# The expert stage of a two-block layer: no subtractions on GpSimd, half the down products in fp32, three tiles' results added by one-hot products ahead of a branch

## The chip, the cores and the metric

One core of a Trainium2 chip runs the whole program: an attention and feed-forward block of two layers, then a second block that ends in a mixture of experts. The metric is the device time of one execution in microseconds. The change touches only the last stage, the experts and what follows them.

## The reference, cut to what matters

512 tokens of width 1024. Each token has one group of four experts and, in it, two experts of inner width 256:

```
g_weight, g_idx = top_k(softmax(x @ w_group + b_group), 1)
e_val, e_idx    = top_k((x @ w_router + b_router)[g_idx], 2)
e_weight        = softmax(e_val) * g_weight
combine[n, e]   = e_weight of expert e for token n, else 0
act = silu(x @ w_gate[e]) * (x @ w_up[e]) * combine[:, e]      # for 16 experts
out = sum over e of act @ w_down[e]
h = h + out;  result = rms_norm(h, norm_final_g)
```

All of it is in float32.

## The kernel before, in words

The kernel computes only the chosen pairs. `route` ranks the 1024 (token, expert) pairs into tiles of 128 rows: tiles 0 to 15 are the first 128 rows of each expert, 16 to 18 hold overflow of experts that got more (their expert is known at run time alone, so their weights come by indirect DMAs that POOL issues), 19 to 22 exist under a branch (`tc.If(rv > 3)`) that these inputs do not take. The order of the tiles is 0 to 9, 16, 17, 18, 10 to 15.

Each tile runs through `moe`: its 128 token rows are gathered from DRAM (`xg`, an indirect DMA of POOL), transposed (`xgp`) and split; six weight chunks of 512 KB (128x1024 floats) come in, four for gate and up, two for down; `up` makes 24 products into one bank (`gups`), ACT applies SiLU (`ma<-gups`), DVE multiplies by weight and up part (`ma`), PE transposes that (`mat`), and `down` makes 12 products (`mdps`). Down of a tile is written after up of the next one.

A product is exact enough only when both sides are split: an fp32 value becomes hi (fp32r, which PE takes in one pass) and lo = value - hi. ACT copies the hi part (`whi`, for down chunks `whx`), a subtraction makes lo (`wlo`, `wlx`), and `mm3` (lines 297 to 299) makes hi*hi, hi*lo and lo*hi. Before the change, of each static tile's six weight subtractions two run on POOL, one of the up chunks and one of the down chunks (in the last tile one in all); the rest are on DVE, for tiles 16 to 18 all six.

The result of a tile (`yt`) is taken from its banks half by ACT, half by DVE (`K.ev` alternates) and written to DRAM (`yb`, an ACT queue DMA). Tiles 14 and 15 (`fin`) are not written: their result stays in SBUF (`yf`, split), and a one-hot matrix `fS` (made by `scatter_from` in the middle of the stage) spreads it over the tokens by products (`fsc`). After the last `moe` step POOL gathers the other results back, eight indirect DMAs of 512 KB (`yg`, one per 128 tokens and choice); then come the branch, the sums into `x` (DVE, POOL, and for two of the token blocks PE through the identity), and the final norm.

Weights are requested 18 chunks ahead (`wstream`) by SP's queue; their buffers are nine `raw` ones and pages of a common pool of 26 (`rawp`, also `xg`, `xgt`, `whx`, `wlx`, `yt`, `yf`, `yg`). A scheduler orders the instructions of each engine by a modelled timeline and inserts the semaphores; on the chip each engine and each DMA queue then runs its list in order. At the branch every engine reads the register and waits for what it needs of the others; nothing is moved across it.

Of the kernel before, what the change touches and what calls it, by code (L numbers as in the profile page):

```python
# [253 lines left out]
class Kern:  # L254
# [1485 lines left out]
    def second_tail(K, mix, xs):  # L1740
        nc, A = K.nc, K.A
        mo = K.pg([128, 512], F32, "moec")
        nc.sync.dma_start(mo, A["moec"])
        wr = K.pg([128, 8, 20], F32, "wrt")
        nc.sync.dma_start(wr.rearrange("p k n -> p (k n)"), A["wrt"])
        nc.gpsimd.tensor_tensor(wr, wr, K.v("gf2").unsqueeze(2).to_broadcast([128, 8, 20]), op=ALU.mult)
        K.eqm = K.rp.tile([128, 256], BF16, name="eqm")
        nc.scalar.activation(K.eqm, mo[:, 128:384], AF.Copy)
        lg = K.rp.tile([128, 4, 20], F32, name="rlg")
        G = K.row(A["grow"][1:2], "gfin")  # L1750
        gf = K.row(A["grow"][0:1], "gf2")
        xnd = K.dp.tile([512, 1024], F32, name="xnd")
        K.yb = [K.dp.tile([n * 128 + 1, 1024], F32, name=f"yb{n}") for n in (17, 4)]
        z = K.pg([1, 1024], F32, "zrow")
        nc.gpsimd.memset(z, 0.0)
        for n, y in zip((17, 4), K.yb):
            nc.scalar.dma_start(y[n * 128:n * 128 + 1, :], z)
        lt = K.bank([128, 4, 20], name="rtp", tag="r")
        K.phase("wout2")
        ws = [K.wconv(t, False) for t in K.w2raw]  # L1760
        ro = K.branch_norm(1)
        K.wstream(5)
        for tb in range(4):
            K.out2(xs[tb], mix, 4, tb, ws, ro[:, tb:tb + 1])
            K.route_in(xs[tb], tb, gf, xnd, wr, lt, lg)
        K.phase('route')
        K.wstream(K.WDEPTH)
        idx, wrow, pos, tl, sl, wsl, nov = K.route(lg, mo)
        K.phase('moe')
        K.wrow = wrow  # L1770
        fin = K.order[-2:]
        S = K.pg([128, 2, 4, 128], F32R, "fS")
        T = {}

        def scatter_from():

            io = mo[:, 0:128]
            for z, j in enumerate(fin):
                m, u = K.rp.tile([128, 2, 4], F32, name=f"fm{z}"), K.rp.tile([128, 4], F32, name=f"fu{z}")
                nc.vector.tensor_scalar(m, tl, float(j), None, op0=ALU.is_equal)  # L1780
                t = K.rp.tile([128, 2, 4], F32, name=f"ft{z}")
                nc.vector.scalar_tensor_tensor(t, sl, 1.0, m, op0=ALU.add, op1=ALU.mult)
                nc.vector.tensor_tensor(u, t[:, 0], t[:, 1], op=ALU.add)
                nc.vector.tensor_scalar(u, u, 1.0, None, op0=ALU.subtract)
# [6 lines left out]
                K.ev(S[:, z], ps)  # L1791
# [12 lines left out]
        def part(ps, tb, h, z):  # L1804
            for p in range(2):
                nc.tensor.matmul(ps, S[:, z, tb], T[z][p][:, h * 512:h * 512 + 512], start=(z == 0 and p == 0), stop=(z == 1 and p == 1 and tb > 1))

        ts = []
        K.moe(K.order, xnd, idx, wsl, K.wnext, fin, T, scatter_from, lambda: ts.extend(gather(0)))
        rv = nc.values_load(nov[0:1, 0:1], min_val=0, max_val=7)  # L1810
        with K.tc.If(rv > 3):
            for j in range(19, 23):
                K.moe([j], xnd, idx, wsl)
            for t in gather(1):
                add(*t)
        for tb in (2, 3):
            nc.gpsimd.tensor_tensor(xs[tb], xs[tb], ts[2 * tb][0], op=ALU.add)
        for tb in range(4):
            t = ts[2 * tb + 1][0]
            if tb > 1:  # L1820
                nc.vector.tensor_tensor(xs[tb], xs[tb], t, op=ALU.add)
            else:
                nc.vector.tensor_tensor(xs[tb], xs[tb], ts[2 * tb][0], op=ALU.add)
            for h in range(2):
                ps = K.bank([128, 512], name="fsc", tag=("T", "g", "b", "T")[tb])
                c = slice(h * 512, h * 512 + 512)
                part(ps, tb, h, 0)
                part(ps, tb, h, 1)
                if tb < 2:
                    nc.tensor.matmul(ps, K.ident, t[:, c], start=False, stop=True)  # L1830
                nc.vector.tensor_tensor(xs[tb][:, c], xs[tb][:, c], ps, op=ALU.add)
        K.phase('final')
        for tb in range(4):
            ss = K.sm([128, 1], "fss")
            K.sumsq(xs[tb], ss)
            r = K.rsqrt(ss, 1, 1.0 / D, EPS, "fr")
            if tb < 0:
                nc.gpsimd.tensor_tensor(xs[tb], xs[tb], G, op=ALU.mult)
                nc.scalar.activation(xs[tb], xs[tb], AF.Copy, scale=r)
            else:  # L1840
                nc.vector.scalar_tensor_tensor(xs[tb], xs[tb], r, G, op0=ALU.mult, op1=ALU.mult)
# [21 lines left out]
    def route(K, lg, mo):  # L1863
# [129 lines left out]
        Z = (17 * 128.0, 4 * 128.0)  # L1993
# [3 lines left out]
        stt(m[:, 0], tl, 13.5, u, op0=ALU.is_lt, op1=ALU.add)  # L1997
        ts(m[:, 1], tl, 18.5, None, op0=ALU.is_gt)
        pi2 = sm([2, 2, 4], "rpos", I32)
        stt(u, u, -256.0, p, op0=ALU.mult, op1=ALU.add)  # L2000
        for z, (q, d) in enumerate(((u, 0.0), (p, 19 * 128.0))):
            stt(m[:, z], q, Z[z] + d, m[:, z], op0=ALU.subtract, op1=ALU.mult)
            ts(pi2[:, z], m[:, z], Z[z], None, op0=ALU.add)
# [21 lines left out]
            K.wq.append((c, j, K.wraw(j, c)))  # L2025
            K.wn += 1

    def wconv(K, raw, pool, pg=False):
        nc = K.nc
        if pg:  # L2030
            hi, lo = K.pg([128, 1024], F32R, "whx"), K.pg([128, 1024], F32R, "wlx")
# [21 lines left out]
    def moe(K, tiles, xnd, idx, wsl, weights=None, fin=(), T=None, mid=None, rest=None):  # L2053

        nc, A = K.nc, K.A
        if not weights:
            def weights(j, cs):
                return [K.wconv(K.wraw(j, c), False) for c in cs]

        def load(j):  # L2060
            x = K.page(j, "xg")
# [19 lines left out]
            nc.vector.scalar_tensor_tensor(a, a, wsl[:, j:j + 1], ps[:, 256:512], op0=ALU.mult, op1=ALU.mult)  # L2081
            return a

        def act(a):
            pt = K.bank([128, 2, 128], name="mat", tag="T")
            for k in range(2):
                nc.tensor.transpose(pt[:, k], a[:, k * 128:k * 128 + 128], K.ident)
            s = K.t2([128, 2, 2, 128], "mas", F32R)
            K.split(s[:, 0], s[:, 1], pt)
            return s  # L2090

        def down(j, s, w):
# [4 lines left out]
            for h in range(2):  # L2097
                c = slice(h * 512, h * 512 + 512)
                ps = K.bank([128, 512], name="mdps", tag="b")
                for k in range(2):  # L2100
                    K.mm3(ps, (s[:, 0, k], s[:, 1, k]), (w[k][0][:, c], w[k][1][:, c]), k == 0, k == 1)
# [12 lines left out]
        for i, j in enumerate(tiles):  # L2114
# [53 lines left out]
```

## Time and profile before

| | |
|---|---|
| time, median of 3 runs | 2298.61 us (2293.86 to 2303.5) |
| the profiled execution | 2302.42 us, span 2300.6 us |
| busy over the span | PE 92%, DVE 64%, ACT 44%, POOL 15% |
| first product of the expert stage | 2043.9 us |
| last up product done | 2257.2 us |
| from there to the end of the span | 43.4 us |

Times in the views are us from the start of the span, durations us unless marked ns. In a timeline the bracket is the idle time of the engine ahead of the instruction and what ended it; "x2" are merged instructions, with one duration over all. PE's products are pipelined, so their starts tell the pace, not their durations. A clock of 1.00 is PE's full speed. `L2036` is line 2036 of the listing.

### The profile page before, as it was taken

The page shows a single profiled execution, that of the slowest core. Times are in us where ns is not written, and L with a number is a line of the kernel's source. Part 1 is how long each engine was busy: PE and PEld are TensorE (multiplying, and loading weights), DVE is VectorE, ACT ScalarE, POOL GpSimd, SP SyncE. Part 2 cuts the span into 40 slices and gives each one's busy share as a digit, 9 for nine tenths or more (in the row PEclk, how much of TensorE's full clock was granted, in tenths as well). Part 3 has the DMA queues.
Part 4 walks back from the last instruction along what each step waited for, and adds up shares of the span by engine and source line. Part 5 has one row for each costly group of instructions (what it writes and reads, how often), then busy time and mean ns, then how long its engine had stood idle before and what let it go on. Part 6 is the DMA issues. An engine that isn't in the chain of part 4 may idle for free. (4 is left out here: it accounts for less than half of the span.)

```text
span 2300.6 us, 30894 instructions
## 1 busy us (share of the span) xinstructions
PE 2126.4 (92%) x11802; PEld 1725.7 (75%) x11802; DVE 1472.3 (64%) x2451; ACT 1013.4 (44%) x1786; POOL 353.0 (15%) x331
## 2 busy tenths in 40 slices
PE   6999998989999999998998989999989998968895
PEld 3777677768888888886876778888867786756673
DVE  4644576567677777767558455565565645669895
ACT  3632562364332232236454464333344544347672
POOL 1300000011010000003100010000001112126744
PEclk8999999979999999998999989999999999979998
DMA  8352022723333344434120432333243345369893
GB/s 334 100 194 81 10 79 103 268 95 106 106 105 125 125 145 160 142 119 147 42 90 18 166 101 83 101 108 94 86 154 90 88 121 172 138 229 352 318 371 121
DMA packets 94394, 321.19 MB, mean 140 GB/s; under 512 B 11262, under 2 KB 12673, under 8 KB 94244
## 3 DMA queue, kind: packets, MB, share of 16 engines
q1 hardware_dynamic: 81472, 280.37, 35.2%
q0 software_dynamic: 10320, 29.89, 4.2%
q10 hardware_dynamic: 2452, 8.92, 1.0%
q8 instruction: 94, 1.54, 0.3%
q14 instruction: 56, 0.46, 0.1%
HBM read 279.39 MB, written 33.46 MB: 136 GB/s over the span
## 5 line engine op out<-in xcount | busy, mean ns | idle before, releaser
L318 DVE TENSOR_TENSOR wlo<-raw,whi 128x1024 fp32r<-128x1024 f32 x200 | 245.4, 1235 | 179.1 <-ACT whi L317 170.0
L317 ACT ACTIVATE whi<-raw 128x1024 fp32r<-128x1024 f32 x200 | 209.9, 1059 | 257.9 <-PE fps L298 194.3
L297 PE MATMUL fps<-h2x,whi 128*128 128x512 f32 x672 | 262.2, 391 | 3.8 <-DVE cvf L702 3.7
L298 PE MATMUL fps<-h2x,whi 128*128 128x512 f32 x672 | 262.5, 391 | 0.0
L299 PE MATMUL fps<-h2x,wlo 128*128 128x512 f32 x672 | 262.0, 391 | 0.0
L1295 DVE TENSOR_TENSOR y<-y,dps 128x512 f32<-128x512 f32 x200 | 134.0, 683 | 108.8 <-PE dps L299 104.1
L1372 POOL TENSOR_TENSOR cvf<-cvf 128x512 f32<-128x512 f32 x66 | 77.1, 1168 | 803.5 <-DVE cvf L702 703.2
L297 PEld LDWEIGHTS fps<-h2x,whi 128*128 128x128 f32 x672 | 126.3, 188 | 31.0 <-ACT whi L317 4.1
L700 ACT ACTIVATE cvf<-fps,cv 128x512 f32<-128x512 f32 (+1 forms) x126 | 87.5, 695 | 139.0 <-PE fps L299 138.9
L299 PEld LDWEIGHTS fps<-h2x,wlo 128*128 128x128 f32 x672 | 126.5, 188 | 27.7 <-issue 1.6
L298 PEld LDWEIGHTS fps<-h2x,whi 128*128 128x128 f32 x672 | 126.7, 188 | 25.8 <-issue 0.4
L298 PE MATMUL dps<-wlo,actx 128*128 128x512 f32 x352 | 137.1, 389 | 0.0
L297 PE MATMUL dps<-whi,actx 128*128 128x512 f32 x352 | 136.6, 390 | 0.3 <-DVE y L1295 0.3
L299 PE MATMUL dps<-whi,actx 128*128 128x512 f32 x352 | 136.6, 389 | 0.0
L420 DVE SCALAR_TENSOR_TENSOR ma<-wm,cs,ma 128x512 f32<-128x512 f32 x140 | 107.7, 814 | 17.4 <-DMA wm<-in_wmod 17.4
L297 PE MATMUL fps<-hx,whi 128*128 128x512 f32 x288 | 113.7, 395 | 0.5 <-ACT v L921 0.5
L299 PE MATMUL fps<-hx,wlo 128*128 128x512 f32 x288 | 113.3, 393 | 0.0
L298 PE MATMUL fps<-hx,whi 128*128 128x512 f32 x288 | 113.2, 393 | 0.0
L701 DVE SCALAR_TENSOR_TENSOR cvf<-fps,cv,cvf 128x511 f32<-128x511 f32 (+1 forms) x126 | 82.5, 655 | 30.2 <-ACT cvf L700 30.0
L297 PE MATMUL fps<-h2c,whi 128*128 128x256 f32 x336 | 96.3, 286 | 4.1 <-ACT cvf L700 4.1
L298 PE MATMUL fps<-h2c,whi 128*128 128x256 f32 x336 | 96.1, 286 | 0.0
L299 PE MATMUL fps<-h2c,wlo 128*128 128x256 f32 x336 | 96.1, 286 | 0.0
(579 smaller groups left out, 5250.3 us busy)
## 6 DMA issues: line engine op xcount, KB each, us to landing
wm<-in_wmod SPq DMA_DIRECT2D x96, 512.0 KB
raw<-in_wup SPq DMA_DIRECT2D x88, 512.0 KB
raw<-in_win SPq DMA_DIRECT2D x52, 512.0 KB
rawp<-in_wexp SPq DMA_DIRECT2D x48, 512.0 KB
raw<-in_wexp SPq DMA_DIRECT2D x48, 512.0 KB
raw<-in_wdown SPq DMA_DIRECT2D x44, 512.0 KB
raw<-in_wout SPq DMA_DIRECT2D x20, 512.0 KB
xd<-xt SPq DMA_DIRECT2D x20, 512.0 KB
```

The lines of the kernel that those rows point to most:

```text
L297: mm(out, st[0], mv[0], start=start, stop=False)
L298: mm(out, st[0], mv[1], start=False, stop=False)
L299: K.lastmm = mm(out, st[1], mv[0], start=False, stop=stop)
L317: nc.scalar.activation(hi, raw, AF.Copy)
L318: (nc.gpsimd if pool else nc.vector).tensor_tensor(lo, raw, hi.bitcast(F32), op=ALU.subtract)
L420: o = nc.vector.scalar_tensor_tensor(a, v, c, a, op0=ALU.mult, op1=ALU.add)
L700: nc.scalar.activation(dst, ps, AF.Identity, scale=w[1], bias=w[3])
L701: nc.vector.scalar_tensor_tensor(dst[:, 1:n], ps[:, 0:n - 1], w[0], dst[:, 1:n], op0=ALU.mult, op1=ALU.add)
L1295: nc.vector.tensor_tensor(y[tb][:, c], y[tb][:, c], pss[hf], op=ALU.add)
L1372: nc.gpsimd.tensor_tensor(t[1], t[0], t[1], op=ALU.mult)
```

## The change

Five edits. POOL makes no weight subtraction any more. In tiles with an odd number the two down chunks are not split: the fp32 chunk itself is the moving side of one fp32 product (`mm1`), with the transposed activation in fp32 (`maf`). The transposes of the activation go to a bank of their own (`r`) instead of sharing `T` with the token transposes. All results that leave by `yt` are taken from the banks by ACT. Three tiles (13, 14, 15) instead of two stay in SBUF; the gathers are issued before the last down, all sums are written ahead of the branch on DVE and PE, and POOL and the identity products have no part in them.

```
-        K.yb = [... for n in (17, 4)]
+        K.yb = [... for n in (16, 4)]
-        fin = K.order[-2:]
+        fin = K.order[-3:]
...
-        def part(ps, tb, h, z):
-            for p in range(2):
-                nc.tensor.matmul(ps, S[:, z, tb], T[z][p][:, h * 512:h * 512 + 512], start=(z == 0 and p == 0), stop=(z == 1 and p == 1 and tb > 1))
+        def part(ps, tb, h):
+            for z in range(3):
+                for p in range(2):
+                    nc.tensor.matmul(ps, S[z][:, tb], T[z][p][:, h * 512:h * 512 + 512], start=(z == 0 and p == 0), stop=(z == 2 and p == 1))
...
         K.moe(K.order, xnd, idx, wsl, K.wnext, fin, T, scatter_from, lambda: ts.extend(gather(0)))
+        for t in ts:
+            add(*t)
+        for tb in range(4):
+            for h in range(2):
+                ps = K.bank([128, 512], name="fsc", tag=("T", "g", "b", "T")[tb])
+                c = slice(h * 512, h * 512 + 512)
+                part(ps, tb, h)
+                nc.vector.tensor_tensor(xs[tb][:, c], xs[tb][:, c], ps, op=ALU.add)
         rv = nc.values_load(nov[0:1, 0:1], min_val=0, max_val=7)
         with K.tc.If(rv > 3):
...
-        for tb in (2, 3):
-            nc.gpsimd.tensor_tensor(xs[tb], xs[tb], ts[2 * tb][0], op=ALU.add)
-        for tb in range(4):
...
-                if tb < 2:
-                    nc.tensor.matmul(ps, K.ident, t[:, c], start=False, stop=True)
-                nc.vector.tensor_tensor(xs[tb][:, c], xs[tb][:, c], ps, op=ALU.add)
...
-        (nc.gpsimd if pool else nc.vector).tensor_tensor(lo, raw, hi.bitcast(F32), op=ALU.subtract)
+        nc.vector.tensor_tensor(lo, raw, hi.bitcast(F32), op=ALU.subtract)
...
-            out.append(K.wconv(raw, j < 16 and c == (2 if j == K.order[-1] else 2 + 3 * (c > 3)), c > 3))
+            out.append((raw,) if c > 3 and j % 2 else K.wconv(raw, c > 3))
...
-        def act(a):
-            pt = K.bank([128, 2, 128], name="mat", tag="T")
+        def act(a, whole):
+            pt = K.bank([128, 2, 128], name="mat", tag="r")
...
+            if whole:
+                s = K.t2([128, 2, 128], "maf")
+                nc.scalar.activation(s, pt, AF.Copy)
...
-                    K.mm3(ps, (s[:, 0, k], s[:, 1, k]), (w[k][0][:, c], w[k][1][:, c]), k == 0, k == 1)
+                    if len(w[k]) == 1:
+                        K.mm1(ps, s[:, k], w[k][0][:, c], k == 0, k == 1)
+                    else:
+                        K.mm3(ps, (s[:, 0, k], s[:, 1, k]), (w[k][0][:, c], w[k][1][:, c]), k == 0, k == 1)
...
-                    K.ev(y[:, c], ps)
+                    nc.scalar.activation(y[:, c], ps, AF.Copy)
...
-        if rest:
-            rest()
+            if rest and i == len(tiles) - 2:
+                rest()
```

POOL's list where the dynamic tiles' weights (`raw` and `rawp` with `rwr`) are requested, before:

```order
L2017 DMA rawp<-in_wexp,rwr 128x1024 x2
L2017 DMA raw<-in_wexp,rwr 128x1024
L2036 TENSOR_TENSOR wlo<-rawp,whi 128x1024
L2017 DMA raw<-in_wexp,rwr 128x1024 x2
L2017 DMA rawp<-in_wexp,rwr 128x1024
L2036 TENSOR_TENSOR wlx<-raw,whx 128x1024
L2062 DMA xg<-xnd,ridx 128x1024
```

and now:

```order
L2052 DMA xg<-xnd,ridx 128x1024 x9
L2007 DMA raw<-in_wexp,rwr 128x1024
L2052 DMA xg<-xnd,ridx 128x1024
L2007 DMA rawp<-in_wexp,rwr 128x1024 x2
L2007 DMA raw<-in_wexp,rwr 128x1024 x2
```

The subtractions that stood between the requests are gone from POOL; only requests are left there.

DVE's list over one tile late in the stage, from the lo part of tile 11's tokens to that of tile 12's, before:

```order
L328 TENSOR_TENSOR xgt_19059<-xgp,xgt_19058 128x512
L2036 TENSOR_TENSOR wlx<-rawp,whx 128x1024
L328 TENSOR_TENSOR mas<-mat,mas 128x256
L2036 TENSOR_TENSOR wlo<-rawp,whi 128x1024
L2036 TENSOR_TENSOR wlo<-raw,whi 128x1024
L2081 SCALAR_TENSOR_TENSOR ma<-ma,rwsl,gups 128x256
L2036 TENSOR_TENSOR wlo<-raw,whi 128x1024
L328 TENSOR_TENSOR xgt_19165<-xgp,xgt_19164 128x512
L923 COPY yt<-mdps 128x512
```

and now the next step, in which the odd tile 11 has its down products (from the tokens of tile 12 to those of tile 13):

```order
L328 TENSOR_TENSOR xgt_19079<-xgp,xgt_19078 128x512 x2
L2026 TENSOR_TENSOR wlo<-rawp,whi 128x1024
L2026 TENSOR_TENSOR wlo<-raw,whi 128x1024
L2026 TENSOR_TENSOR wlo<-rawp,whi 128x1024
L2071 SCALAR_TENSOR_TENSOR ma<-ma,rwsl,gups 128x256
L2026 TENSOR_TENSOR wlo<-raw,whi 128x1024
L328 TENSOR_TENSOR xgt_19176<-xgp,xgt_19175 128x512 x2
```

The third `wlo` has come from POOL; the `wlx`, the `mas` and the `yt` of this step have left DVE. With an even tile's down it has two `wlx` and one `mas` more.

PE's list at the end, before, from tile 15's down products to the sums behind the branch, which these inputs jump over (19552 and 19553 are hi and lo of tile 14, 19602 and 19603 of tile 15):

```order
L2087 MATMUL mat<-ident,ma 128x128 x2
L297 MATMUL mdps<-whx,mas 128x512 x2
...
L1810 TENSOR_LOAD rnov
L1811 COMPARE_AND_BRANCH
...
L1806 MATMUL fsc<-yf_19552,fS 128x512
L1806 MATMUL fsc<-yf_19553,fS 128x512
L1806 MATMUL fsc<-yf_19602,fS 128x512
L1806 MATMUL fsc<-yf_19603,fS 128x512
```

and now (19364 and 19365 are tile 13, 19450 and 19451 tile 14, 19475 and 19476 tile 15; the branch follows the last of these products):

```order
L2077 MATMUL mat<-ident,ma 128x128 x2
L1808 MATMUL fsc<-yf_19364,fS_17593 128x512
L1808 MATMUL fsc<-yf_19365,fS_17593 128x512
L1808 MATMUL fsc<-yf_19450,fS_17593 128x512 x4
L302 MATMUL mdps<-rawp,maf 128x512
L302 MATMUL mdps<-raw,maf 128x512
L1808 MATMUL fsc<-yf_19451,fS_17593 128x512 x2
```

The one-hot products now begin ahead of tile 15's down products, which are four fp32 ones (`L302`), and all stand ahead of the branch.

## Rows read from the trace of the kernel before

**Rows 1.** Busy time by window: us, busy (instructions) by engine, granted clock, DMA share, GB/s.

```profile
2050.00:2070.00 20.00, 17.13 (x70) 13.18 (x69) 14.08 (x16) 14.87 (x21) 9.36 (x5) 0.83 0.70 253
...
2070.00:2110.00 40.00, 35.53 (x170) 28.15 (x168) 38.91 (x32) 29.54 (x39) 27.37 (x12) 1.00 0.94 347
...
2170.00:2230.00 60.00, 54.63 (x259) 42.59 (x258) 55.53 (x56) 44.52 (x62) 26.13 (x13) 1.00 1.03 414
```

**Rows 2.** Timeline, ACT: start, us; the SiLU that follows each tile's last up product.

```profile
2054.31 0.39 ACT L2080 ACTIVATE ma<-gups 128x256 f32<-128x256 f32 x1
...
2105.46 0.38 ACT L2080 ACTIVATE ma<-gups 128x256 f32<-128x256 f32 x1 [0.25 <-PE gups L299]
...
2121.76 0.39 ACT L2080 ACTIVATE ma<-gups 128x256 f32<-128x256 f32 x1 [0.24 <-PE gups L299]
...
2193.63 0.39 ACT L2080 ACTIVATE ma<-gups 128x256 f32<-128x256 f32 x1 [0.30 <-PE gups L299]
...
2203.07 0.38 ACT L2080 ACTIVATE ma<-gups 128x256 f32<-128x256 f32 x1 [0.25 <-PE gups L299]
...
2257.21 0.38 ACT L2080 ACTIVATE ma<-gups 128x256 f32<-128x256 f32 x1 [3.71 <-PE gups L299]
```

**Rows 3.** Groups by line, 2043.9 to 2257.2: busy, mean ns | idle before, releasers.

```profile
L2036 DVE TENSOR_TENSOR wlo<-raw,whi 128x1024 fp32r<-128x1024 f32 x36 | 68.5, 1902 | 3.5 <-ACT whi L2035 3.1 <-DMA raw<-in_wexp 0.5
...
L2036 DVE TENSOR_TENSOR wlo<-rawp,whi 128x1024 fp32r<-128x1024 f32 x21 | 41.1, 1957 | 8.5 <-ACT whi L2035 8.5
...
L2036 DVE TENSOR_TENSOR wlx<-raw,whx 128x1024 fp32r<-128x1024 f32 x3 | 3.6, 1212 | 0.0
...
L2036 POOL TENSOR_TENSOR wlo<-rawp,whi 128x1024 fp32r<-128x1024 f32 x15 | 38.8, 2585 | 28.7 <-ACT whi L2035 17.7 <-issue 10.9
...
L2036 POOL TENSOR_TENSOR wlx<-raw,whx 128x1024 fp32r<-128x1024 f32 x15 | 36.7, 2446 | 46.5 <-ACT whx L2035 41.1 <-issue 5.3
...
L298 PE MATMUL mdps<-wlx,mas 128*128 128x512 f32 x68 | 25.4, 405 | 4.7 <-POOL wlx L2036 4.7
...
L2087 PE MATMUL mat<-ident,ma 128*128 128x128 f32 x36 | 8.1, 310 | 9.4 <-DVE xgt L328 9.1 <-DVE ma L2081 0.3
```

**Rows 4.** Timeline at a dynamic tile: POOL's subtraction, PE's wait in brackets.

```profile
2159.45 2.35 POOL L2036 TENSOR_TENSOR wlx<-raw,whx 128x1024 fp32r<-128x1024 f32 x1
...
2161.85 0.79 PE L298 MATMUL mdps<-wlx,mas 128*128 128x512 f32 x1 [3.22 <-POOL wlx L2036]
```

**Rows 5.** Timeline, PE: two fp32r products of 512 columns.

```profile
2230.20 0.40 PE L298 MATMUL gups<-wlo,xgt 128*128 128x512 f32 x1
...
2230.43 0.40 PE L299 MATMUL gups<-whi,xgt 128*128 128x512 f32 x1
```

**Rows 6.** Timeline, PE weight loads: one half of an fp32 product of 512 columns.

```profile
2275.51 0.19 PEld L1830 LDWEIGHTS fsc<-yg,ident 128*128 128x128 f32 x1 [0.24 <-issue]
```

**Rows 7.** Timeline of the end, all engines.

```profile
2252.91 0.33 ACTq L2108 DMA_DIRECT2D yb<-yt  x1
...
2258.39 0.96 POOL L1797 DMA_INDIRECT yg<-yb,rpos  x1 [2.18 <-DVE ma L2081]
...
2262.14 1.70 POOL L1797 DMA_INDIRECT yg<-yb,rpos  x1 [0.30 <-DMA yg<-yb,rpos]
...
2265.87 1.29 DVE L328 TENSOR_TENSOR yf<-mdps,yf 128x512 fp32r<-128x512 f32 x2 [1.70 <-issue]
...
2268.62 2.36 DVE L1823 TENSOR_TENSOR x<-x,yg 128x1024 f32<-128x1024 f32 x2 [1.47 <-DMA yg<-yb,rpos]
...
2276.59 4.71 POOL L1817 TENSOR_TENSOR x<-x,yg 128x1024 f32<-128x1024 f32 x2 [7.77 <-DMA yg<-yb,rpos]
...
2282.97 1.87 DVE L1831 TENSOR_TENSOR x<-x,fsc 128x512 f32<-128x512 f32 x3
...
2286.11 1.06 ACT L466 ACTIVATE junk<-x 128x1024 bf16<-128x1024 f32 x1
...
2291.55 0.55 POOL L336 TENSOR_TENSOR frr<-frs,mhalf 128x1 f32<-128x1 f32 x1 [1.46 <-DVE frs L334]
```

More of the change, by code (lines that the diff above doesn't have):

```diff
@@ L1752, in second_tail @@
         xnd = K.dp.tile([512, 1024], F32, name="xnd")
-        K.yb = [K.dp.tile([n * 128 + 1, 1024], F32, name=f"yb{n}") for n in (17, 4)]
+        K.yb = [K.dp.tile([n * 128 + 1, 1024], F32, name=f"yb{n}") for n in (16, 4)]
         z = K.pg([1, 1024], F32, "zrow")
         nc.gpsimd.memset(z, 0.0)
-        for n, y in zip((17, 4), K.yb):
+        for n, y in zip((16, 4), K.yb):
             nc.scalar.dma_start(y[n * 128:n * 128 + 1, :], z)
@@ L1759, in second_tail @@
         K.phase("wout2")
-        ws = [K.wconv(t, False) for t in K.w2raw]
+        ws = [K.wconv(t) for t in K.w2raw]
         ro = K.branch_norm(1)
@@ L1770, in second_tail @@
         K.wrow = wrow
-        fin = K.order[-2:]
-        S = K.pg([128, 2, 4, 128], F32R, "fS")
+        fin = K.order[-3:]
+        S = [K.pg([128, 2, 4, 128], F32R, f"fS{z}") for z in range(2)]
+        S = [S[z // 2][:, z % 2] for z in range(3)]
         T = {}
@@ L1790, in scatter_from @@
                     nc.tensor.transpose(ps[:, b], o[:, b], K.ident)
-                K.ev(S[:, z], ps)
+                K.ev(S[z], ps)
         def gather(z):
@@ L1815, in second_tail @@
                 add(*t)
-        for tb in (2, 3):
-            nc.gpsimd.tensor_tensor(xs[tb], xs[tb], ts[2 * tb][0], op=ALU.add)
-        for tb in range(4):
[L1819 to L1828, printed above, removed]
-                if tb < 2:
-                    nc.tensor.matmul(ps, K.ident, t[:, c], start=False, stop=True)
-                nc.vector.tensor_tensor(xs[tb][:, c], xs[tb][:, c], ps, op=ALU.add)
         K.phase('final')
@@ L1836, in second_tail @@
             r = K.rsqrt(ss, 1, 1.0 / D, EPS, "fr")
[L1837 to L1841, printed above, removed]
+            nc.vector.scalar_tensor_tensor(xs[tb], xs[tb], r, G, op0=ALU.mult, op1=ALU.mult)
             nc.sync.dma_start(K.out[tb * 128:tb * 128 + 128, :], xs[tb])
@@ L1992, in route @@
         p, u, m = sm([2, 4], "rpp"), sm([2, 4], "rpu"), sm([2, 2, 4], "rpm")
-        Z = (17 * 128.0, 4 * 128.0)
+        Z = (16 * 128.0, 4 * 128.0)
         stt(p, tl, 128.0, sl, op0=ALU.mult, op1=ALU.add)
@@ L1996, in route @@
         stt(u, tl, 18.5, u, op0=ALU.is_lt, op1=ALU.mult)
-        stt(m[:, 0], tl, 13.5, u, op0=ALU.is_lt, op1=ALU.add)
+        stt(m[:, 0], tl, 12.5, u, op0=ALU.is_lt, op1=ALU.add)
         ts(m[:, 1], tl, 18.5, None, op0=ALU.is_gt)
         pi2 = sm([2, 2, 4], "rpos", I32)
-        stt(u, u, -256.0, p, op0=ALU.mult, op1=ALU.add)
+        stt(u, u, -384.0, p, op0=ALU.mult, op1=ALU.add)
         for z, (q, d) in enumerate(((u, 0.0), (p, 19 * 128.0))):
@@ L2026, in wstream, with wconv @@
             K.wn += 1
-    def wconv(K, raw, pool, pg=False):
+    def wconv(K, raw, pg=False):
         nc = K.nc
@@ L2057, in weights @@
             def weights(j, cs):
-                return [K.wconv(K.wraw(j, c), False) for c in cs]
+                return [K.wconv(K.wraw(j, c)) for c in cs]
         def load(j):
@@ L2082, in up @@
             return a
-        def act(a):
-            pt = K.bank([128, 2, 128], name="mat", tag="T")
+        def act(a, whole):
+            pt = K.bank([128, 2, 128], name="mat", tag="r")
             for k in range(2):
                 nc.tensor.transpose(pt[:, k], a[:, k * 128:k * 128 + 128], K.ident)
-            s = K.t2([128, 2, 2, 128], "mas", F32R)
-            K.split(s[:, 0], s[:, 1], pt)
+            if whole:
+                s = K.t2([128, 2, 128], "maf")
+                nc.scalar.activation(s, pt, AF.Copy)
+            else:
+                s = K.t2([128, 2, 2, 128], "mas", F32R)
+                K.split(s[:, 0], s[:, 1], pt)
             return s
@@ L2100, in down @@
                 for k in range(2):
[L2101 removed]
+                    if len(w[k]) == 1:
+                        K.mm1(ps, s[:, k], w[k][0][:, c], k == 0, k == 1)
+                    else:
+                        K.mm3(ps, (s[:, 0, k], s[:, 1, k]), (w[k][0][:, c], w[k][1][:, c]), k == 0, k == 1)
                 if j in fin:
@@ L2104, in down @@
                 else:
-                    K.ev(y[:, c], ps)
+                    nc.scalar.activation(y[:, c], ps, AF.Copy)
             if j not in fin:
-                z, r = (0, j - 2 * (j > 15)) if j < 19 else (1, j - 19)
+                z, r = (0, j - 3 * (j > 15)) if j < 19 else (1, j - 19)
                 nc.scalar.dma_start(K.yb[z][r * 128:r * 128 + 128, :], y)
@@ L2122, in moe @@
                 down(*prev)
-            prev = (j, act(a), weights(j, (4, 5)))
+            v = weights(j, (4, 5))
+            prev = (j, act(a, len(v[0]) == 1), v)
             if mid and i == 4:
                 mid()
-        if rest:
-            rest()
+            if rest and i == len(tiles) - 2:
+                rest()
         down(*prev)
```

## The prediction

> **What bounds the kernel now.** I began with the order lists of the two kernels: up to the routing they are the same, so only the last 257 us of the 2300.6 us span can change. I read these in two parts, the stage of 19 tiles and what follows its last up product, because different things end last in them.
>
> For the stage I took the busy time by window first. Between 2170 and 2230 us PE is busy 54.6 of 60 us at clock 1.00, DVE 55.5, and the DMA engines are full at 414 GB/s; between 2070 and 2110 DVE is busy 38.9 of 40 us and DMA runs at 347 GB/s [rows 1]. No engine alone explains the pace, so I measured it: ACT's SiLU follows the last up product of each tile. From the first (2054.31) to the last (2257.21) it is 202.9 us for 18 tiles, 11.3 us each; the fastest tile took 9.44 us (2193.63 to 2203.07), the one in the middle that carries `scatter_from` 16.3 us (2105.46 to 2121.76), the last five 10.8 us each [rows 2]. POOL made one subtraction in the fast tile and two in each of the last ones.
>
> Then the groups by line say what stands between 9.4 and 11 us. A weight subtraction on DVE takes 1.21 us where POOL rests, but the 57 of `wlo` average 1.92 us (68.5 + 41.1 us over 36 + 21), and POOL needs 2.45 to 2.59 us for each of its 30 [rows 3]. So POOL's help of 30 x 1.21 = 36 us of DVE time costs DVE 57 x 0.71 = 40 us in stretched instructions. PE feels it: its transposes `mat` wait 9.4 us behind DVE, and the down products 4.7 us for POOL itself [rows 3]. The worst place is among the dynamic tiles, where POOL's subtraction stands behind the DMA requests: it starts at 2159.45 and PE idles 3.22 us for it [rows 4].
>
> After the last up product (E, 2257.2 us) the chain is: the result of tile 13 is requested to DRAM at 2252.91, POOL starts the gathers at 2258.39, POOL's first sum waits 7.77 us for gathered rows until 2276.59, DVE adds bank by bank, POOL's last power starts at 2291.55, and the span ends 9.05 us after that [rows 7].
>
> **The change in the stage.** I build the time of 18 tiles afresh from the fastest tile, since its 9.44 us is about PE's own work and POOL was least in the way.
>
> Subtractions. DVE will make 96 instead of 83 in all, of which 93 fall in the stage: 93 x 1.21 = 113 us against 68.5 + 41.1 + about 27 for the 21 `wlx`, that is 136 us; an engine that was full gets 23 us of room, and the evictions of `yt` leave it too. They go to ACT, which was busy 44.5 of 60 us [rows 1] and loses two conversions in each odd tile, so I cost them at nothing; their cover is gone if ACT comes to be as full as DVE was. So the 9.44 us hold for all: 18 x 9.44 = 169.9 us. The bounds: the 10.8 us of the last five tiles on one side (nothing gained), no better than 9.44 on the other, since PE is then never idle.
>
> fp32 down products. PE passes 512 columns in 0.23 us in fp32r [rows 5]; one fp32 product is two instructions of 0.43 us each (0.19 busy and 0.24 idle on the weight side) [rows 6]. An odd tile has 4 x 0.86 = 3.44 us in place of 12 x 0.23 = 2.76: 0.7 us more on PE, which is on the path. Eight odd tiles have their down products inside the stage: +5.6 us. It goes no lower, as no row has the fp32 product quicker.
>
> Rest of the stage. The third one-hot matrix and six one-hot products that now run before E: 1.9 us. The middle step cost 16.3 - 11.0 = 5.3 us over a plain tile [rows 2]; DVE is free of POOL there but builds three matrices, I keep 2.0 (bounds 0 and 8, half as much again as before). PE's clock of 0.83 in the first 20 us [rows 1] costs 0.17 x 16 = 2.7 us, as before. For hand-overs between PE, ACT and DVE I keep 0.3 us a tile, 5.4 us, near half of what `mat` lost; and 1 us for the dynamic tiles. Sum: 169.9 + 5.6 + 1.9 + 2.0 + 2.7 + 5.4 + 1.0 = 188.5 us against 202.9: -14.4 us. The bounds are -25 us (no hand-over, no middle step, and the dynamic tiles clean) and 0. The separate bank for `mat` I cost at nothing: one buffer suffices for a transpose per tile, and its price without cover is the wait for one split, under 1 us a tile.
>
> The one subtraction that moves to DVE during routing stands where its neighbours were stretched by POOL; with the third tile's small instructions I take +0.5 us (0 to 1.5).
>
> **The change after E.** The gathers no longer wait for the late tiles. Tile 12's result is out about 16 us before E, so by the 5.5 us from request to first gather [rows 7] the first one starts near E - 10, and as the last rows landed 18.2 us after the first request before (2258.39 to 2276.59, an upper bound), they are there by E + 8. On PE: 15 products of 0.23 us and the transposes of tile 15 (4.1 us), eight one-hot and four fp32 products (5.3), 34 one-hot products (7.8): E + 17.2. On DVE, one instruction behind the other from E + 0.9: eight gathered sums of 1.18 us, four lo parts of 0.65, eight sums from banks of 0.62 [rows 7] and the activation: 17.5 us, E + 18.4 with small waits; I take 18.2. The branch costs 1.46 us from DVE's last instruction (2265.87 + 1.29) to its next (2268.62) [rows 7]; it was under the gathers before, and is bare now. Then four sums of squares of 1.06 us and their read-out on ACT, about 1.2 each, and the last scaling factor behind two writes of DVE of 1.3: some 7.1 us to POOL's last power, and 9.05 to the end. E + 35.8 against E + 43.4: -7.6 us (bounds -11, if the sums do not wait for one another, and 0, if the gathers come late).
>
> A rule weighed here. Beside two DVE subtractions one gather request took 1.70 instead of 0.96 us [rows 7], so I let each of the eight grow by at most 0.75 us, 6 us in all, and they still land at E + 14, when DVE needs the last of them. The Trainium skill (SBUF — State Buffer, "SBUF: two separate sides") says that a DVE instruction on the shared port pair keeps GpSimd from writing descriptors until it ends. By that rule each request could wait for a whole 1.21 us subtraction, 9.7 us in all, and the end would come some 4 us later than in my sum; the row shows a smaller price.
>
> **The sum.** -14.4 - 7.6 + 0.5 = -21.5 us. The profiled execution took 2302.4 us, 1.8 us more than its span and 3.8 us above the median of the runs, and would come to 2280.9; from the median it is 2277.
>
> **The rivals.**
> 1. The weights set the pace. From 2050 to 2240 us some 64 MB move. At 414 GB/s that is 155 us, at 347 GB/s 185 us [rows 1], the last weights at 2235 and E 10 to 18 us later, so the stage gains 4 to 12 us. For it: the DMA share is 0.94 to 1.03 in these windows. Against: PE's waits in [rows 3] name DVE and POOL, not transfers. With the end as above: 2298.6 - 8 - 7.1 = 2283.5, down to 2287 with a slow end.
> 2. The stage gains only what fp32 takes: POOL's subtractions were covered but for the 4.7 us in [rows 3], and 5.6 us are added. Then just the end is left: 2298.6 - 7.6 = 2291. For it: PE was already busy 54.6 of 60 us [rows 1]. Against: the 9.44 us tile.
> 3. Slower: the fp32 chunks of odd tiles stay in their `raw` buffers until their down products are done, about half a tile (5 us) longer. SP's queue is in order, so the chunk that waits for such a buffer holds up all behind it. If nothing absorbs it, 8 x 5 = 40 us come on top: 2277 + 40 = 2317. It decides from the point where more than half of that reaches PE, that is when fewer than some three of the 18 chunks requested ahead have landed. Against it: whole pages of hi and lo parts are no longer taken for these tiles, and DVE waited only 0.5 us for landings [rows 3].
>
> **How the numbers follow.** What a measurement here tells from no change is about 0.5%, 11.5 us, that is from 2287 to 2310. The forecast has 0.60, with 2268 to 2287 as its own range; rival 1 0.14; rival 2 0.16; rival 3 0.10, of which 0.03 would come out within the half per cent. Faster gets 0.59 of the forecast, 0.12 of rival 1 and 0.06 of rival 2, 0.77; no change 0.01 + 0.02 + 0.10 + 0.03 = 0.16; slower 0.07. The range has the forecast's bounds below (-33 us, of which the last part is unlikely) and rival 2 above: 2266 to 2293.
>
> **What would show it.** In the profile after: all weight subtractions of DVE near 1.21 us and PE's waits for POOL gone; tiles about 9.6 us apart with even and 10.3 with odd down products, and E near 2243; the fp32 products at 0.43 us an instruction; gathers under way before E; sums ended some 18 us after E, and 36 us from E to the end. Rival 1 would show as DVE and ACT waiting for `raw` landings, rival 3 as SP waiting for PE's down products. The forecast is wrong if the tiles stay near 10.8 us, or if the end takes over 40 us.

## The result, and the profile after

The changed kernel took 2272.3 us (median of 4 runs, 2270.2 to 2276.1) against 2298.9 us: ratio 0.9886, 95% interval 0.9867 to 0.9904, so 26.6 us less where 21.5 were forecast.

The two profiled spans differ by more, 2300.6 against 2268.4 us. Part of that belongs to neither kernel: 8.6 us of it are there before the routing, where both execute the same instructions (the first product of the expert stage came at 2043.9 us before and at 2036.7 us after; over all profiles below it lies between 2035.9 and 2049.3). From the routing on the trace gives +1.4 us up to the first product, -16.7 from there to the last up product E (213.2 to 196.5 us), and -8.3 from E to the end (43.5 to 35.2): -23.6 us.

The table of busy time by window has these rows for the changed kernel (columns as in [rows 1]); the last is the whole stretch from the first product to E:

```profile
2070.00:2110.00 40.00, 38.52 (x171) 28.69 (x170) 28.67 (x33) 26.44 (x40) 4.39 (x3) 0.96 1.01 392
...
2150.00:2210.00 60.00, 56.59 (x250) 41.33 (x249) 45.94 (x52) 45.50 (x67) 6.51 (x6) 1.00 1.03 411
...
2036.68:2233.22 196.54, 188.58 (x824) 139.62 (x824) 146.45 (x164) 141.40 (x202) 50.54 (x42) 0.99 0.91 349
```

The same stretch before, and the two eighths of it with the lowest clock but for the first:

```profile
2043.94:2257.17 213.23, 188.09 (x850) 147.48 (x850) 183.50 (x172) 148.99 (x200) 121.63 (x64) 0.95 0.83 310
...
2097.24:2123.90 26.66, 22.50 (x106) 17.91 (x105) 23.58 (x22) 16.98 (x23) 14.67 (x7) 0.94 0.89 334
...
2150.55:2177.21 26.66, 20.46 (x86) 15.56 (x85) 20.55 (x19) 14.27 (x20) 21.01 (x16) 0.87 0.93 329
```

PE is now busy 96% of the stretch, was 88%; DVE has fallen from 86 to 75%. DMA moves 392 GB/s where it moved 347 [rows 1]. PE's busy time is equal in both although the fp32 products were added: before, its granted clock was 0.95 on average (a mean of its two levels, 1.2 and 2.4 GHz), and a product lasted longer.

ACT's SiLU after the last up product of each tile, as in [rows 2]:

```profile
2046.59 0.38 ACT L2070 ACTIVATE ma<-gups 128x256 f32<-128x256 f32 x1
...
2090.74 0.39 ACT L2070 ACTIVATE ma<-gups 128x256 f32<-128x256 f32 x1
...
2106.92 0.38 ACT L2070 ACTIVATE ma<-gups 128x256 f32<-128x256 f32 x1 [0.32 <-PE gups L299]
...
2203.76 0.39 ACT L2070 ACTIVATE ma<-gups 128x256 f32<-128x256 f32 x1 [0.32 <-PE gups L299]
...
2212.31 0.38 ACT L2070 ACTIVATE ma<-gups 128x256 f32<-128x256 f32 x1 [0.27 <-PE gups L299]
...
2223.94 0.38 ACT L2070 ACTIVATE ma<-gups 128x256 f32<-128x256 f32 x1 [0.32 <-PE gups L299]
...
2233.26 0.38 ACT L2070 ACTIVATE ma<-gups 128x256 f32<-128x256 f32 x1 [2.93 <-issue]
```

186.7 us for 18 tiles, forecast 188.5. The steps are uneven (8.6 and 11.6 us in the two shown), so the pairs count, about 10.1 us a tile. The middle step still takes 16.2 us.

The groups by line, from the first product to E, that answer to [rows 3]:

```profile
L2026 DVE TENSOR_TENSOR wlo<-raw,whi 128x1024 fp32r<-128x1024 f32 x36 | 44.0, 1222 | 1.8 <-ACT whi L2025 0.8 <-issue 0.2
L2026 DVE TENSOR_TENSOR wlo<-rawp,whi 128x1024 fp32r<-128x1024 f32 x36 | 44.0, 1222 | 34.3 <-ACT whi L2025 28.6 <-issue 5.4
...
L2077 PE MATMUL mat<-ident,ma 128*128 128x128 f32 x36 | 7.1, 279 | 1.8 <-DVE ma L2071 1.8
```

All 72 `wlo` at 1.22 us, `mat` waits 1.8 us where it waited 9.4. Nothing in PE's waits names POOL any more; the largest (line waited for: us in total, times, longest) are

```profile
PE gups L299 <- DVE xgt L328: 2.4, 4, 0.6
PE mat L2077 <- DVE ma L2071: 1.8, 4, 0.6
PE fsp L1791 <- DVE fo L1787: 1.3, 1, 1.3
PE gups L297 <- ACT xgt L327: 1.3, 3, 0.8
...
PE gups L297 <- DMA rawp<-in_wexp: 0.2, 1, 0.2
```

The fp32 halves start 0.43 us apart, as in [rows 6], here on the weight side in the stage:

```profile
2195.47 0.19 PEld L302 LDWEIGHTS mdps<-raw,maf 128*128 128x128 f32 x1 [0.24 <-issue]
...
2195.90 0.19 PEld L302 LDWEIGHTS mdps<-raw,maf 128*128 128x128 f32 x1 [0.24 <-issue]
```

The timeline of the end, against [rows 7]; E is 2233.2:

```profile
2221.32 1.27 POOL L1798 DMA_INDIRECT yg<-yb,rpos  x1 [15.51 <-DMA yb<-yt]
...
2234.07 2.48 DVE L1803 TENSOR_TENSOR x<-x,yg 128x1024 f32<-128x1024 f32 x2
...
2248.07 3.11 DVE L1819 TENSOR_TENSOR x<-x,fsc 128x512 f32<-128x512 f32 x5
...
2252.64 1.06 ACT L466 ACTIVATE junk<-x 128x1024 bf16<-128x1024 f32 x1 [9.65 <-DVEq L1821]
...
2259.29 0.54 POOL L336 TENSOR_TENSOR frr<-frs,mhalf 128x1 f32<-128x1 f32 x1 [2.15 <-DVE frs L334]
```

Gathers from E - 11.9 on, gathered rows never waited for, sums done at E + 18.0 (2248.07 + 3.11), the branch's 1.46 us bare, the last power at E + 26.1.

### The profile page after: what moved, and what is told of

Same layout as the page of the kernel before. It is cut to its first block, busy times and chain, and to the rows that moved or that the text cites. A ratio compares the mean times of both kernels' runs of the same rounds, so it can differ in the third digit from the quotient of the medians.

```text
span 2268.4 us, 30778 instructions
## 1 busy us (share of the span) xinstructions
PE 2116.6 (93%) x11778; PEld 1710.1 (75%) x11778; DVE 1434.2 (63%) x2449; ACT 1003.2 (44%) x1786; POOL 262.7 (12%) x298
## 5 line engine op out<-in xcount | busy, mean ns | idle before, releaser
L318 DVE TENSOR_TENSOR wlo<-raw,whi 128x1024 fp32r<-128x1024 f32 x200 | 245.6, 1237 | 181.0 <-ACT whi L317 172.0
```

## The experiments

The ratios are against the kernel before on the same chip, whose median was 2298.8 us beside runs 1 to 4 and 9 and 10, 2297.1 beside 5 to 8 and 2297.4 beside 11 and 12. "Stage" is the stretch from the first product to E, "end" from E to the end, both in the one profiled execution of each kernel. They leave out the part ahead of the stage, which wanders by several us from one execution to the next, but one execution says nothing of its own spread.

| run | us | ratio (95%) | stage | end |
|---|---|---|---|---|
| before | 2298.9 | 1 | 213.2 | 43.5 |
| changed | 2272.3 | 0.9886 (0.9867 to 0.9904) | 196.5 | 35.2 |
| 1 before, no POOL subtractions | 2274.7 | 0.9893 (0.9877 to 0.9910) | 189.9 | 42.1 |
| 2 changed, no fp32 | 2274.9 | 0.9904 (0.9887 to 0.9920) | 193.5 | 38.0 |
| 3 changed, fp32 in all static tiles | 2279.0 | 0.9920 (0.9903 to 0.9936) | 197.1 | 35.1 |
| 4 changed, old end | 2280.3 | 0.9928 (0.9911 to 0.9944) | 194.6 | 40.7 |
| 5 changed, POOL subtracts again | 2301.9 | 1.0015 (1.0002 to 1.0028) | 220.0 | 35.9 |
| 6 before, new end | 2300.9 | 1.0013 (1.0001 to 1.0026) | 220.3 | 41.4 |
| 7 changed, fp32 in tile 15 only | 2269.3 | 0.9881 (0.9863 to 0.9900) | 189.7 | 35.0 |
| 8 as 7, old bank and evictions | 2267.5 | 0.9870 (0.9853 to 0.9886) | 189.8 | 35.0 |
| 9 as 1, POOL repeats in quarters | 2342.6 | 1.0192 (1.0172 to 1.0212) | 257.9 | 44.0 |
| 10 as 8, two tiles | 2266.5 | 0.9864 (0.9844 to 0.9883) | 187.0 | 37.2 |
| 11 as 1, POOL repeats | 2329.5 | 1.0147 (1.0124 to 1.0170) | 245.5 | 43.6 |
| 12 as 1, POOL subtracts landed chunks | 2301.9 | 1.0017 (1.0002 to 1.0031) | 216.8 | 41.2 |

**Run 1.** Of the kernel before:

```
-            out.append(K.wconv(raw, j < 16 and c == (...), c > 3))
+            out.append(K.wconv(raw, False, c > 3))
```

> The kernel before with one edit: every weight subtraction on DVE, none on POOL. Theory: POOL's help cost more than it gave; DVE's own clean work in the stage is then 72 x 1.22 + 36 x 1.22 + about 57 us of other work = 189 us, so DVE sets the pace and the stage falls from 205 to about 195 us: ratio to before 0.995, some 2288 us, wlo at 1.22 us, PE waiting for DVE. Rival: without the room that the fp32 down products make, taking POOL's 30 subtractions onto DVE only lengthens the stage: 2300 to 2310 us.

2274.7 us, the way of the theory but further than its 2288. This one edit gives the stage 23.3 us and nearly the whole of the time. DVE does not set the pace by itself, as the theory had it: its busy time in the stage is 173.7 us, not 189. Its `wlo`, PE's wait that was 9.1 us in [rows 3], and the busy time over the stage:

```profile
L2036 DVE TENSOR_TENSOR wlo<-raw,whi 128x1024 fp32r<-128x1024 f32 x36 | 44.0, 1221 | 1.5 <-ACT whi L2035 1.3
L2036 DVE TENSOR_TENSOR wlo<-rawp,whi 128x1024 fp32r<-128x1024 f32 x36 | 43.9, 1220 | 5.5 <-ACT whi L2035 5.5
...
PE mat L2087 <- DVE xgt L328: 0.3, 1, 0.3
```

```profile
2097.00:2215.00 118.00, 114.09 (x545) 90.10 (x543) 112.07 (x132) 92.51 (x130) 36.77 (x30) 1.00 1.02 410
2049.28:2239.19 189.91, 182.61 (x850) 144.51 (x850) 173.73 (x202) 146.11 (x200) 41.92 (x36) 0.98 0.88 347
```

In the middle 118 us PE (114), DVE (112) and DMA (share 1.02) are all full, and nothing waits long. PE's idle time in the stage falls from 25.1 to 7.3 us, that is 17.8; the other 5.5 of the 23.3 us are in the PE column of the second row: the same 850 products as before take 182.6 us instead of 188.1. Before, the clock fell to 0.94 and 0.87 in the eighths with the middle step and the dynamic tiles, in which PE stood longest; so part of the waits was paid twice.

**Run 2.** Of the changed kernel:

```
-            out.append((raw,) if c > 3 and j % 2 else K.wconv(raw, c > 3))
+            out.append(K.wconv(raw, c > 3))
```

> The changed kernel with all down products made from split parts again (no fp32 ones), POOL still without subtractions. Theory that the changed stage is paced by PE (busy 182 of 190 us): PE does 8 x 0.7 = 5.5 us less, DVE 16 x 1.22 + 8 x 0.4 = 23 us more (166 of 190), ACT 17 us more (155): still covered, 2267 to 2273 us. Rival that the fp32 products pay by the conversions they save: DVE and ACT fall behind and the time goes to 2278 to 2285 us.

2274.9 us, between the two. The trace tells why it is not decided by the time: one token gather came late and PE stood 3.3 us for it, with the low clock behind it (tile 18 took 16.9 us):

```profile
2162.81 1.06 PE L2061 MATMUL xgp<-ident,xg 128*128 128x128 f32 x8 [3.34 <-DMA xg<-xnd,ridx]
```

The end is 3 us longer, since tile 15's down chunks are now subtracted by DVE among the sums. The stage is 3 us shorter all the same. So neither side of the expectation is decided here; runs 7 and 8 come back to it.

**Run 3.** `j < 16` in place of `j % 2` in that line.

> The changed kernel with fp32 down products in all 16 static tiles, not only in the odd ones. Theory that PE paces the stage: 7 more tiles x 0.7 us before the last up product and one after, so 2277 us, +5. Rival that conversions and hand-overs pace it: DVE loses 23 us and ACT 17, the time falls to 2262 to 2270 us.

+6.7 us in the median, the way that PE as the pace said. The stage of the one profile is only 0.6 us longer, but that execution was the quickest of the four by 6 us (2272.6 against 2278.7 to 2282.1).

**Run 4.** The stage's edits on the code of before, with its end.

> The changed kernel with the end of the kernel before: two tiles by one-hot products, gathers after the last step, sums behind the branch on DVE, POOL and PE. Theory: the stage keeps its gain, the end takes 43 us from the last up product instead of 35, and 2 us of one-hot products leave the stage: 2278 to 2280 us. Rival that the early gathers, issued by POOL beside the last tiles, cost the stage what they save at the end: 2270 to 2274 us.

2280.3 us, so the new end is worth 8.0 us in the median on the changed stage, as the theory said. The profile shows less: the stage is 1.9 us longer with it (2 expected) and the end 5.5 us shorter (8 expected).

**Runs 5 and 6.** The changed kernel with POOL's subtractions, and the kernel before with the new end alone:

```
-            out.append((raw,) if c > 3 and j % 2 else K.wconv(raw, c > 3))
+            out.append((raw,) if c > 3 and j % 2 else K.wconv(raw, c > 3, j < 16 and c == (2 if j == K.order[-1] else 2 + 3 * (c > 3))))
...
-        nc.vector.tensor_tensor(lo, raw, hi.bitcast(F32), op=ALU.subtract)
+        (nc.gpsimd if pool else nc.vector).tensor_tensor(lo, raw, hi.bitcast(F32), op=ALU.subtract)
```

> The changed kernel with POOL's subtractions put back (one up chunk of each static tile, one down chunk of each even static one). Theory that POOL's help is what cost the stage: wlo on DVE goes back to 1.7 to 1.9 us, PE waits for POOL and DVE again, the first-to-last stretch grows from 196.5 to about 210 us: 2283 to 2290 us. Rival that it hurt before only because DVE was full, which it no longer is with the fp32 down products: 2270 to 2276 us.

> The kernel before with the new end alone (three tiles by one-hot products, gathers before the last down, sums ahead of the branch), POOL's subtractions kept. Theory: the end gains 8 us, 2.7 us of one-hot products come into the stage: 2292 to 2295 us. Rival that the early gathers stand on POOL among its late subtractions and are delayed by them: no gain, 2297 us or more.

Run 5: 2301.9 us, everything is lost again, more than expected, although DVE is not full at all (149 of 220 us busy). `wlo` is stretched, and PE waits for what stands in POOL's queue as well:

```profile
L2026 DVE TENSOR_TENSOR wlo<-raw,whi 128x1024 fp32r<-128x1024 f32 x36 | 63.1, 1752 | 8.4 <-ACT whi L2025 7.3 <-issue 0.6
```

```profile
PE gups L299 <- DVE xgt L328: 6.5, 7, 2.1
PE xgp L2061 <- DMA xg<-xnd,ridx: 5.7, 2, 4.2
PE gups L298 <- POOL wlo L2026: 3.8, 1, 3.8
```

Run 6: 2300.9 us, no gain, as the rival said. E is at 2256.2, the first gather leaves POOL only half a us ahead of it, behind POOL's last subtraction, and the first sum waits for its rows:

```profile
2252.34 3.24 POOL L2026 TENSOR_TENSOR wlx<-raw,whx 128x1024 fp32r<-128x1024 f32 x1 [5.15 <-ACT whx L2025]
2255.73 0.96 POOL L1798 DMA_INDIRECT yg<-yb,rpos  x1
...
2260.04 1.23 DVE L1803 TENSOR_TENSOR x<-x,yg 128x1024 f32<-128x1024 f32 x1 [2.94 <-DMA yg<-yb,rpos]
```

The end gains 2 us instead of 8, and the stage loses 7, of which 5.2 are one late token gather (PE's wait for `xg`). The late gathers cost the end the 2.9 us of that wait. Another 3 are missing because tile 15's down chunks are split here, as in run 2, whose end is 38.0 with early gathers. And POOL need not be free: in run 5 it subtracts, its first gather leaves 3.1 us ahead of E, the first sum waits 1.0 us, and the end is still 35.9. So the new end is worth its gain when its first rows are there for the first sum and tile 15 has fp32 down products.

**Runs 7 and 8.** The line of run 2 with `j == 15` in place of `j % 2`; run 8 with two more lines put back:

```
-            pt = K.bank([128, 2, 128], name="mat", tag="r")
+            pt = K.bank([128, 2, 128], name="mat", tag="T")
...
-                    nc.scalar.activation(y[:, c], ps, AF.Copy)
+                    K.ev(y[:, c], ps)
```

> The changed kernel with the fp32 down products in tile 15 alone, whose down products stand after the last up product. Theory: PE loses the 4 us that fp32 costs before that point (7 odd tiles), and the end stays at 35 us: 2267 to 2270 us, if no token gather is late (one was in the variant with none in fp32, 3.3 us of waiting and the low clock behind it). Rival that the conversions of the other odd tiles cost DVE and ACT more than PE gains: 2274 us or more.

> The kernel before with only two of the five edits, no POOL subtractions and the new end, and fp32 in tile 15 alone: the transposes share the bank T again, half of the evictions of yt are on DVE. Theory (PE sets the pace, these two edits are worth nothing): 190 us first to last as with no POOL subtractions alone, plus 2.7 for the third tile, and an end of 35: 2266 to 2269 us. Rival that DVE, busy 187 of 190 us without POOL, is now too full and delays the end: 2273 us or more.

Both times as the theory, 2269.3 and 2267.5 us. The stage falls to 189.7 and 189.8 us, the same as in run 1, and the end stays at 35.0: in the profiled stages fp32 in the other odd tiles (eight, since tile 17 is one) cost 6.8 us, and the bank and the evictions were worth nothing. About half of the 6.8 us lies in the middle step, which takes 13.8 to 16.2 us in the changed kernel and runs 3 and 4 and 12.2 to 12.9 in runs 1, 2, 7, 8 and 10. The device times do not show it: the ratio is 0.9881 for run 7 and 0.9870 for run 8 against the changed kernel's 0.9886, with intervals that overlap. That they are faster rests on the stages of single executions. Nor is DVE as full without POOL as the expectations have it: 174 us of the stage in run 1 and 175 in run 8, not 187.

**Run 10.** Run 8 with `fin = K.order[-2:]` and the positions that go with it.

> The best version so far (no POOL subtractions, sums ahead of the branch, fp32 in tile 15 alone) with two tiles by one-hot products in place of three. Theory: 16 one-hot products less, of which PE saves up to 3.7 us and DVE 1.3 (two lo parts), but the gathers wait for tile 13's result, some 10 us later, so the last rows land near the last sums: 2264 to 2268 us. Rival that the end now waits for the gathers: the end grows from 35 to 38 us or more and the time is 2269 to 2273.

2266.5 us, as the theory; in the profiles the stage is 2.8 us shorter than in run 8 and the end 2.2 longer. The third tile is an even exchange.

**Runs 9, 11 and 12.** What did POOL's subtractions cost by themselves? Run 1, with POOL doing work whose results nothing reads. Run 9 makes four pieces of 256 columns of each subtraction, run 11 one of 1024 (the first line below), run 12 reads a landed chunk four places ahead instead (the second):

```
+                K.nc.gpsimd.tensor_tensor(K.idle, raw, out[-1][0].bitcast(F32), op=ALU.subtract)
+                K.nc.gpsimd.tensor_tensor(K.idle, K.wq[3][2], K.wq[3][2], op=ALU.subtract)
```

> No POOL subtractions in the real work (all on DVE, as in the first experiment), but POOL makes the same 31 subtractions of the same chunks once more, each as four of 256 columns into a buffer that nothing reads, so PE and DVE never wait for a result of POOL. Theory that POOL's work itself hurts, by stretching DVE's instructions beside it and by holding up the token gathers in its queue: wlo mean back to 1.8 or 1.9 us, DVE already full, 2295 to 2315 us. Rival that only the lateness of POOL's results hurt (PE waiting for wlo and wlx made there): 2273 to 2280 us as without POOL.

Far over either expectation, and not a clean test: four pieces took 4.5 us instead of 2.5, and they held the few `whi` buffers, for which ACT waited 55 us:

```profile
L2036 ACT ACTIVATE whi<-raw 128x1024 fp32r<-128x1024 f32 x36 | 37.9, 1054 | 48.8 <-POOL idle L2049 42.7 <-PE gups L299 6.1
L2036 ACT ACTIVATE whi<-rawp 128x1024 fp32r<-128x1024 f32 x36 | 37.9, 1052 | 16.8 <-POOL idle L2049 12.7 <-PE gups L299 3.9
```

> As the first experiment (all real subtractions on DVE), and POOL makes 31 of them once more at the same chunks as in the kernel before, one instruction of 1024 columns each (some 2.4 us) into a page that nothing reads (one page less for the rest). POOL reads the hi buffer as it did before, but nobody waits for its result. Theory that POOL's work beside DVE is the price, whatever its results are for: wlo at 1.7 to 1.9 us on DVE, which was already busy 187 of 190 us, 2300 to 2315 us. Rival that what cost was PE waiting for results that POOL made late: 2274 to 2282 us.

> As the run above, but POOL's 30 subtractions read only a weight chunk that has landed and waits for its turn, four chunks ahead, so that no hi buffer is held by POOL and nobody waits for its result; what is left is POOL's traffic beside DVE and the token gathers behind it in POOL's queue. Theory of the shared memory side: wlo again at 1.6 to 1.9 us and 2295 to 2310 us. Rival that the buffers which POOL reads late were the price (in the run with four pieces ACT waited 55 us for POOL to release them): wlo near 1.25 us and 2274 to 2282 us.

Run 11 is worse than both expectations, still with 18.7 us of ACT waiting for buffers that POOL held. Run 12 has no such wait, no result of POOL is awaited, and it is 27.2 us slower than run 1 in the median, 26.9 in the stage. Its rows:

```profile
L2037 DVE TENSOR_TENSOR wlo<-raw,whi 128x1024 fp32r<-128x1024 f32 x36 | 52.0, 1445 | 0.5 <-ACT whi L2036 0.5
...
L2037 DVE TENSOR_TENSOR wlx<-raw,whx 128x1024 fp32r<-128x1024 f32 x18 | 32.1, 1783 | 0.0
...
L2048 POOL TENSOR_TENSOR idle<-raw 128x1024 f32<-128x1024 f32 x15 | 35.5, 2365 | 11.3 <-DMA raw<-in_wexp 9.8 <-SPq L1812 1.0
```

```profile
PE mat L2091 <- DVE xgt L328: 15.5, 12, 2.4
```

37 of DVE's 108 subtractions lie beside one of POOL's and last 2.11 us on average, the other 71 last 1.21: 33 us of stretch. PE's largest wait is again for DVE (15.5 us, 0.3 in run 1); for a token gather behind POOL's subtractions it waits once, 2.7 us. The run also takes one page from the pool, and no run shows what that costs alone. In the kernel before, 43 of DVE's subtractions lay beside POOL's, at 2.19 us, against 35 at 1.22: 41.7 us lost on DVE to be spared 30 x 1.22 = 36.6. POOL's help was worth less than nothing, by the stretch alone; PE's waits for POOL's results, 5.5 us (4.7 of them in [rows 3]), came on top.

## Why the prediction was right, point by point

- **Subtractions.** The part without POOL can be checked by run 1: the forecast's terms but for fp32 (5.6) and the one-hot products (1.9) are 188.5 - 7.5 = 181.0 us; run 1 took 179.1 from SiLU to SiLU. The size was right, and the exchange of 36 us for 40 us that it read from the `wlo` rows is borne out: 36.6 for 41.7 by the trace of before, and run 12 shows the stretch with POOL's results out of play. The reason that an engine that was full gets room was not right: DVE is fuller in run 1 (173.7 of 189.9 us against 183.5 of 213.2), and that is the quicker stage. What went away there is PE's waiting for stretched and late work.
- **What was luck.** The plain tile came out at about 10.0 us (run 8, with DVE and DMA full beside PE), not at 9.44 and 0.3 for hand-overs, and the middle step cost more than its term. Against that the first step took 5.9 us, less than a plain tile, and the 2.7 us for the low clock at the start hardly arose: the granted clock of the stage's first eighth was 0.95, where it had been 0.81. That the sum of the stage came within 2 us is owed in part to these errors cancelling.
- **fp32 down products.** Forecast +5.6; 0.43 us an instruction was right, and run 7 against the changed kernel gives 6.8 us in the profiled stages. What was seen as a price for relieving DVE bought nothing there. It pays in tile 15 alone, whose conversions stand after E: the end is 38.0 us without it and 35.0 with it.
- **The third tile.** 1.9 us for the stage; run 8 against run 10 gives 2.8.
- **The middle step.** 2.0 us over a plain tile was too little: 16.2 against some 9.5 is 6.7, within the bounds of 0 and 8. Without fp32 in the odd tiles it is about 3 (12.5 in run 7). PE waits 1.3 us for the one-hot matrix there.
- **Hand-overs and dynamic tiles.** 6.4 us forecast together; PE's idle stretches from the first product to E add up to 8.0 (7.3 in run 1, 25.1 before).
- **Bank and evictions.** Nothing, as forecast (run 8 against run 7).
- **Routing.** +1.4 against +0.5, within its bounds.
- **The end.** E + 35.2 against E + 35.8. First request at E - 11.9 (E - 10), sums at E + 18.0 (18.2), the branch 1.46, 8.1 from the sums to the last power where 7.1 was forecast, 9.1 behind it. But the term was counted as if it were the gathers' and sums' own: without fp32 products in tile 15 the end is 3 us longer (run 2), and with gathers that leave only at E it is longer again (run 6).
- **The rule on descriptors.** The eight requests took 0.93 to 1.55 us each, 1.8 us over their shortest in all, and the last was issued 1.4 us ahead of E. Nothing waited for the gathered rows, so neither the row's price nor the rule's could show in the time. But the row was misread: it does not show a smaller price than the rule's. The 1.70 us in [rows 7] are the 0.89 us that DVE's subtraction still had to run and 0.81 more, which is the rule; the last section has this over all runs.
- **The rivals.** Weights as the pace: over the stage DMA moved 349 GB/s, 310 before, with a full stretch of 411 where 414 had been reached already, and PE waited 0.2 us for a landing; in runs 1 and 8 DMA is one of three full engines, so the next gain may meet it. Covered POOL subtractions: refuted by runs 1, 5 and 12. Held `raw` buffers: SP waited 9.8 us in all for the fp32 down products, but neither DVE nor ACT waited for weights to land.

Left open is how the last 3 us between the traces' sum (-23.6) and the medians (-26.6) come about; they are within the interval, and executions differ by more ahead of the stage.

## What to carry to other kernels

Price an engine's help by what it does to its neighbours' instructions, not only by what it takes off them: take one group's mean where the helper works and where it rests. Here the help did not even break even, and what waited for the stretched work and for the helper's results made it a loss of 24 us. And where a bundle of edits wins, undo each one: here one edit made nearly all of the gain, the new end paid only with the others beside it, and fp32 paid in the last tile alone; in the others the profiled stages show a cost.

## What the runs showed of the hardware

POOL's subtraction and DVE's don't share, they exclude one another. In the kernel before, one of POOL's from 2080.33 to 2082.98:

```profile
2080.33 2.65 POOL L2036 TENSOR_TENSOR wlx<-raw,whx 128x1024 fp32r<-128x1024 f32 x1 [3.62 <-ACT whx L2035]
...
2080.64 0.41 DVE L328 TENSOR_TENSOR mas<-mat,mas 128x256 fp32r<-128x256 f32 x1
...
2081.24 2.83 DVE L2036 TENSOR_TENSOR wlo<-rawp,whi 128x1024 fp32r<-128x1024 f32 x1 [0.18 <-ACT whi L2035]
```

`wlo`, whose two inputs are both in SBUF, ends at 2084.07, 1.09 us after POOL's instruction: it did its work once that was over. `mas`, with one input in PSUM, takes its 0.41 us beside it. It is so without exception: in the stage of the kernel before, each of the 25 DVE subtractions that took over 1.3 us ends 1.07 to 1.10 us after one of POOL's, as do the 23 of run 12. The other way round, a POOL subtraction that begins while one of DVE's runs ends 2.24 to 2.34 us after that one; the longest took 3.21 us. The 11 `mas` and 11 `ma` beside a POOL subtraction take 0.41 and 0.47 us like the others. The longest `wlo` of the kernel before:

```profile
2143.19 3.80 DVE L2036 TENSOR_TENSOR wlo<-raw,whi 128x1024 fp32r<-128x1024 f32 x1 [0.20 <-ACT whi L2035]
...
2143.54 2.36 POOL L2036 TENSOR_TENSOR wlx<-raw,whx 128x1024 fp32r<-128x1024 f32 x1
```

The Trainium skill (SBUF — State Buffer, "SBUF: two separate sides") states this as a lock: a DVE instruction with two SBUF inputs and a GpSimd one that reads SBUF hold the port pair in turn, each for its whole length. The trace agrees, with these numbers; which of two that start close together goes first, it does not tell by the start times (the `wlo` above starts 0.35 us ahead of POOL's instruction and still waits for it).

POOL's gather requests are held in the same way. In run 6, the slowest one:

```profile
2264.98 1.22 DVE L1803 TENSOR_TENSOR x<-x,yg 128x1024 f32<-128x1024 f32 x1
...
2265.05 1.96 POOL L1798 DMA_INDIRECT yg<-yb,rpos  x1 [0.30 <-issue]
```

The sum has 1.15 us left when the request begins, and the request ends 0.81 us after it. Of the 112 requests for result rows in the 14 traces, 35 begin with at least 0.14 us of such a DVE instruction (a weight subtraction or a sum of gathered rows) left to run, and each ends 0.80 to 0.84 us after it. The other 77 take 0.93 to 0.96 us.
